# A two-layer diffusion block: the token stages put in source order, with the scan rewritten as a pipeline

## The chip, the cores and the metric

The kernel runs on one core of a Trainium2 chip. A core has a matrix engine (PE, whose weight loads are listed as PEld), a vector engine (DVE), a scalar engine (ACT), a general engine (POOL) and an engine that here only issues transfers (SP); each runs its own list of instructions from the first to the last, and they meet through semaphores. SBUF is the core's working memory, PSUM holds the matrix engine's sums. The metric is device microseconds of one execution.

## The reference, cut to what matters

Two layers are computed over 1024 latent and 256 context tokens of width 1024. Per layer:

```python
u = rmsnorm(h, g_pre) * (1 + sc) + sh                 # modulated, latent and context
p = split_proj(u @ w_in)                              # xbc, z, dt | gq gk gv gg | dq dk dv dg
y_s = ssd(p)       # xs,B,C = silu(dwconv(xbc)); scan in both directions, chunks of 128:
                   #   y_diag = (C B^T . exp(segsum(dt a))) (x dt)     inside a chunk
                   #   S_next = S * exp(sum dt a) + B (decay x dt)     state between chunks
                   #   y_off  = C S exp(cumsum dt a)                   state into the chunk
                   # y = yf + flip(yb) + x * d_skip; rmsnorm(y * silu(z)) * norm_g
y_g = attention(rope(norm(gq)), rope(norm(gk)), gv) * silu(gg)
y_d = norm(att(q1, k1, v) - lam * att(q2, k2, v)) * silu(dg)
h = h + gate * rmsnorm(concat(y_s, y_g, y_d) @ w_out, g_post)
```

The second layer needs no context output. All is float32 in and out; products are made of a high and a low part of each factor, so that one product is three matmuls.

## The kernel before, in words

The 1280 tokens are ten tiles of 128 (0 and 1 are context). Each layer goes through a stage with features on partitions (the convolution's channels), a **token stage**, the attention and the output projection. This text is about the token stage: 206 to 603 us in the first layer, 1273 to 1614 us in the second.

In it the rest of `w_in` is multiplied tile by tile, in five column blocks that the code calls chunks, in the order 0 (z), 1 (q and k of the differential attention), 3 (its v, 256 wide), 2 (q, k, v of the grouped attention), 4 (the gates); the others are 512 wide. A tile's product is eight k-steps of three matmuls into a PSUM tile `prj` (L958 to L960); `tok_chunk` first loads a chunk's weights and splits them (`wh`, `wl`), and then takes each tile from `prj` to `raw` (L977) and on: rotary (L879 to L888), in chunk 2 also a norm (squares L895, sums L897, an inverse root on POOL L117, the multiplication L899), the split in two parts `st` (L830 to L834), transposes `qps` (L841) and the store. In chunks 0 and 4 a tanh gate `th` (L963, L964) is stored through a ring of two buffers (`gt` or `z`, L965).

Beside chunks 0, 1 and 3 runs `scan()`, whose `yield`s are taken 1.3 times per 512-wide product. Per scan chunk it loads `xbf`, `ab` and `bct`; makes `gp` (L767) and from it `gf`; two DVE operations per head make the decay D (L773, L774), ACT its exponential (L776); eight copies on ACT (L779) and eight DVE operations (L780) make W, POOL multiplies W by D (L782), and PE multiplies by x (`pd`, L790). The state of either direction is decayed in place on POOL (L718), increased by `stp` (L714, L720) and read by `po` (L726, scaled L728). Outputs of the two directions are added when the second one comes to a tile, through partial sums in DRAM (`d_yp`, then `d_ys`). `finish()` (L731) reads that sum and z, and does gate, norm, transposes and the store; it is called on every second tile of chunks 2 and 4.

What stands in the program in this way is only a set of priorities: the whole kernel is put in order by a list scheduler, which simulates the engines and takes at each point the ready instruction with the best priority. On every engine the order is then fixed.

Of the kernel before, what the change touches and what calls it, by code (L numbers as in the profile page):

```python
# [48 lines left out]
SCR = 1.3  # L49
# [18 lines left out]
def block_kernel(ctx: ExitStack, tc: tile.TileContext, tok, cvec, wmod, pack,  # L68
# [61 lines left out]
    def cs(c):  # L130
        return slice(c * P, (c + 1) * P)
# [297 lines left out]
    for l in range(DEPTH):  # L429
# [15 lines left out]
        d_yp = dp.tile([NT, P, 512], F32, name=f"yp{l}")  # L445
        d_ys = dp.tile([NT, P, 512], F32, name=f"ys{l}")
# [8 lines left out]
        pk = lt_([P, NPK - NPM], "pk")  # L455
# [249 lines left out]
        def state_step(c, dr, xb, S, first):  # L705

            xs = sp.tile([P, 2, 256], F32, name="xs", tag="xs")
            G.tensor_tensor(xs.rearrange("p g (h d) -> p g h d", h=4),
                            xb[:, :, 0:256].rearrange("p g (h d) -> p g h d", h=4),
                            coef[:, dr, c, :].rearrange("p (g h) -> p g h", g=2).unsqueeze(3)  # L710
                            .to_broadcast([P, 2, 4, 64]), op=ALU.mult)
            ps = xpp.tile([P, 2, 256], F32, name="stp", tag="st")
            for g in range(2):
                TE.matmul(ps[:, g], xb[:, g, 256:384], xs[:, g], start=True, stop=True)  # L714
            if first:
                V.tensor_copy(S, ps)
            else:
                G.tensor_tensor(heads(S.rearrange("p g x -> p (g x)")), heads(S.rearrange("p g x -> p (g x)")),  # L718
                                per_head(etot, dr, c), op=ALU.mult)
                V.tensor_add(S, ps, S)  # L720

        def y_off(c, dr, bc, S):
# [4 lines left out]
            yt = sp.tile([P, 512], F32, name="yt", tag="yt")  # L727
# [3 lines left out]
        def finish(c, fp, nb=2):  # L731

            y = fp.tile([P, 512], F32, name="yf", tag="yf", bufs=nb)
            SY.dma_start(y, d_ys[c])
            zt = fp.tile([P, 512], F32, name="zt", tag="zt", bufs=nb)
            SY.dma_start(zt, d_z[c])
            V.tensor_tensor(y, y, zt, op=ALU.mult)
            sa = small.tile([P, 1], F32, name="sa")
            S_.activation(zt, y, AF.Square, accum_out=sa)
            rr = inv_root(sa, [P, 1], 1.0 / 512, 4 * EPS, "s")  # L740
            V.tensor_scalar(y, y, rr, None, op0=ALU.mult)
            pt = trp.tile([P, 4, P], F32, name="ytp", tag="tr")
            for i in range(4):
                TE.transpose(pt[:, i], y[:, cs(i)], ident)
            z3 = zt.rearrange("p (k t) -> p k t", k=4)
            V.tensor_tensor(z3, pt, pc("ssdg").unsqueeze(2).to_broadcast([P, 4, P]), op=ALU.mult)
            yp = fp.tile([P, 4, 2, P], F32R, name="yp2", tag="yp2", bufs=1)
# [4 lines left out]

        def scan():
            half = set()
            Sf = sp.tile([P, 2, 256], F32, name="Sf")
            Sb = sp.tile([P, 2, 256], F32, name="Sb")
            for c, cb in enumerate((1, 0, 9, 8, 7, 6, 5, 4, 3, 2)):
                xb = sp.tile([P, 2, 384], F32, name="xbf", tag="xb", bufs=2)
                SY.dma_start(xb, d_xb[c])
                if c >= t0:  # L760
                    ab = sp.tile([P, 2, 8, P], F32, name="ab", tag="ab")
                    SY.dma_start(ab, d_acs[:, c].unsqueeze(0).to_broadcast([P, 2, 8, P]))
                    bc = sp.tile([P, 4, P], F32, name="bct", tag="bct", bufs=2)
                    SY.dma_start(bc, d_bc[:, :, cs(c)].rearrange("i p t -> p i t"))
                    pg = xpp.tile([P, 2, P], F32, name="gp", tag="gp")
                    for g in range(2):
                        TE.matmul(pg[:, g], bc[:, 2 * g], bc[:, 2 * g + 1], start=True, stop=True)  # L767
                    gf = sp.tile([P, 2, 2, P], F32, name="gf", tag="gf")
                    V.tensor_tensor(gf[:, 0], pg, mge.unsqueeze(1).to_broadcast([P, 2, P]), op=ALU.mult)
                    V.tensor_tensor(gf[:, 1], pg, mle.unsqueeze(1).to_broadcast([P, 2, P]), op=ALU.mult)  # L770
                    D, W = ab[:, 0], ab[:, 1]
# [5 lines left out]
                    yield  # L777
                    for h in range(8):
                        S_.activation(W[:, h], gf[:, 0, h // 4], AF.Copy, scale=dts[:, 0, c, h:h + 1])  # L779
                        V.scalar_tensor_tensor(W[:, h], gf[:, 1, h // 4], dts[:, 1, c, h:h + 1], W[:, h],  # L780
                                               op0=ALU.mult, op1=ALU.add)
                    G.tensor_tensor(W, W, D, op=ALU.mult)  # L782
                    y = sp.tile([P, 512], F32, name="y", tag="y", bufs=2)
                    G.tensor_tensor(y.rearrange("p (g h d) -> p g h d", g=2, h=4),
                                    xb[:, :, 0:256].rearrange("p g (h d) -> p g h d", h=4),
                                    pc("dskip").rearrange("p (g h) -> p g h", g=2).unsqueeze(3)
                                    .to_broadcast([P, 2, 4, 64]), op=ALU.mult)
                    pd = xpp.tile([P, 8, 64], F32, name="pd", tag="pd")
                    for h in range(8):
                        TE.matmul(pd[:, h], W[:, h], xb[:, h // 4, h % 4 * 64:h % 4 * 64 + 64],  # L790
                                  start=True, stop=True)
                    V.tensor_tensor(y, pd.rearrange("p h d -> p (h d)"), y, op=ALU.add)
                    if c:
                        yt = y_off(c, 0, (bc[:, 1], bc[:, 3]), Sf)
                        G.tensor_tensor(y, yt, y, op=ALU.add)
                    if c in half:
                        yt = sp.tile([P, 512], F32, name="yp", tag="yp")
                        SY.dma_start(yt, d_yp[c])
                        G.tensor_tensor(y, yt, y, op=ALU.add)
                    whole = c in half or c == 1  # L800
                    half.add(c)
                    SY.dma_start((d_ys if whole else d_yp)[c], y)
                    yield
                if c != NT - 1:
                    state_step(c, 0, xb, Sf, c == 0)
                xb = sp.tile([P, 2, 384], F32, name="xbb", tag="xb", bufs=2)
                SY.dma_start(xb, d_xb[cb])
                if c and cb >= t0:
                    ct = sp.tile([P, 2, P], F32, name="ct", tag="ct")
                    SY.dma_start(ct, d_bc.rearrange("(g b) p t -> b p g t", b=2)[1][:, :, cs(cb)])  # L810
                    yt = y_off(cb, 1, (ct[:, 0], ct[:, 1]), Sb)
                    if cb in half:
                        y = sp.tile([P, 512], F32, name="y", tag="y", bufs=2)
                        SY.dma_start(y, d_yp[cb])
                        G.tensor_tensor(y, yt, y, op=ALU.add)
                        SY.dma_start(d_ys[cb], y)
                    else:
                        half.add(cb)
                        SY.dma_start(d_yp[cb], yt)
                if cb != 2:  # L820
                    state_step(cb, 1, xb, Sb, c == 0)
# [68 lines left out]
        def gqa_norm(ck, raw, parts, t):  # L890
# [3 lines left out]
            sq = ck.tile([P, nh, 64], F32, name="gsq", tag="t2", bufs=T2B)  # L894
            S_.activation(sq, raw3, AF.Square)  # L895
# [13 lines left out]
        with pool("rot") as rp, pool("tokc", 2) as ck:  # L909
# [29 lines left out]
            def tok_chunk(ck, ch, first):  # L939
# [11 lines left out]
                for t in range(first, NT):  # L951
# [26 lines left out]
                    if ch == 1:  # L978
                        if t >= 2:
                            rope(ck, raw, 16, 16, cosd[:, t - 2], nsind[:, t - 2], sind[:, t - 2], False)  # L980
# [641 lines left out]
```

## Time and profile before

| | |
|---|---|
| median of 3 runs | 2064.58 us (2062.05 to 2068.44) |
| profiled execution, its own time | 2063.46 us |
| its span in the trace | 2061.6 us |
| mean granted clock of PE | 0.937 |
| busy in the span | PE 88%, PEld 71%, DVE 69%, POOL 59%, ACT 51% |
| token stages | 397.1 us in layer 0, 341.6 us in layer 1 |

The stages are cut at these times: chunks 0, 1 and 3 with the scan, then chunk 2, then chunk 4. In the stage view a line gives the stretch, its length, the busy time of PE, PEld, DVE, ACT and POOL with the number of instructions, then the granted clock of PE (1.00 is its upper level), the busy share of the transfer engines and GB/s. In a list of waits a line says which instruction stood and for which, the total, the number of times and the longest one. A name such as `ab` is a tile of the program.

### The profile page before, as it was taken

To read this page: it belongs to the slowest core of one execution; us is meant where nothing else is said; L and a number is where in the kernel's file an instruction comes from. 1 tells how busy PE (TensorE), PEld (TensorE's weight loads), DVE (VectorE), ACT (ScalarE), POOL (GpSimd) and SP (SyncE) were. 2 spreads that over 40 slices of the span, in tenths; PEclk is the share of its full clock that TensorE was granted. 3 is DMA by queue.
4 is the path that set the end of the run, shared out by engine and by line. 5 is a ranking of instruction groups with operands and counts; after the bars stand their busy time and mean duration, and the time that the engine had idled before them with its cause. 6 is when DMAs were issued, how large, how long until landed. Compare 5 with 4: busy or idle time off the path is not lost. (4 is left out here: it accounts for less than half of the span.)

```text
span 2061.6 us, 30333 instructions
## 1 busy us (share of the span) xinstructions
PE 1806.6 (88%) x9936; PEld 1471.4 (71%) x9936; DVE 1428.5 (69%) x3286; ACT 1041.5 (51%) x1955; POOL 1211.7 (59%) x1135
## 2 busy tenths in 40 slices
PE   4899989899879999988988799888899899989895
PEld 3677777787668667876775487777777777878783
DVE  4777566766538776698866578468656588788954
ACT  3445233334437775766654345234244477777661
POOL 3626245747616676777755326466567378787761
PEclk9899999899999999998989899999999999999897
DMA  9157546776786788786656138667766866557545
GB/s 290 47 170 271 152 165 191 236 235 176 222 259 198 245 263 257 234 256 202 211 191 214 63 102 280 226 183 231 244 202 204 260 185 192 157 155 237 161 152 205
DMA packets 359998, 418.57 MB, mean 203 GB/s; under 512 B 38753, under 2 KB 252833, under 8 KB 359841
## 3 DMA queue, kind: packets, MB, share of 16 engines
q1 hardware_dynamic: 359840, 416.64, 65.1%
q8 instruction: 78, 1.28, 0.3%
q14 instruction: 80, 0.65, 0.1%
HBM read 282.18 MB, written 134.38 MB: 202 GB/s over the span
## 5 line engine op out<-in xcount | busy, mean ns | idle before, releaser
L128 POOL TENSOR_TENSOR pl<-pf,ph 128x512 fp32r<-128x512 f32 x283 | 373.6, 1325 | 189.0 <-DVE ph L1391 69.7
L1241 DVE TENSOR_SCALAR_CACHE_REDUCE pt<-sc 128x512 f32<-128x512 f32 (+1 forms) x600 | 334.2, 587 | 78.5 <-PE sc L1239 63.4
L958 PE MATMUL prj<-wh,u 128*128 128x512 f32 (+1 forms) x768 | 296.6, 389 | 33.0 <-DVE th L964 18.1
L1254 ACT ACTIVATE pt<-pt,nm 128x1280 f32<-128x1280 f32 x192 | 262.3, 1366 | 92.1 <-DVE nm L1252 91.0
L959 PE MATMUL prj<-wl,u 128*128 128x512 f32 (+1 forms) x768 | 294.8, 384 | 10.3 <-POOL wl L128 7.8
L960 PE MATMUL prj<-wh,u 128*128 128x512 f32 (+1 forms) x768 | 291.7, 380 | 0.0
L1369 PE MATMUL tp<-ident,pt 128*128 128x128 f32 x1312 | 209.3, 285 | 14.0 <-ACT pt L1254 5.6
L1379 ACT COPY pf<-tp 128x512 f32<-128x512 f32 x289 | 166.8, 581 | 74.9 <-PE tp L1369 49.3
L1412 PE MATMUL po<-pl,vt 128*128 128x256 f32 x644 | 183.1, 307 | 15.6 <-POOL pl L128 14.7
L958 PEld LDWEIGHTS prj<-wh,u 128*128 128x128 f32 x768 | 151.8, 199 | 62.5 <-DVE th L964 19.9
L1411 PE MATMUL po<-ph,vt 128*128 128x256 f32 x644 | 186.0, 303 | 5.2 <-DVE ph L1391 2.9
L1369 PEld LDWEIGHTS tp<-ident,pt 128*128 128x128 f32 x1312 | 162.1, 147 | 37.9 <-ACT pf L1379 10.7
L959 PEld LDWEIGHTS prj<-wl,u 128*128 128x128 f32 x768 | 152.0, 198 | 38.0 <-POOL wl L128 11.2
L960 PEld LDWEIGHTS prj<-wh,u 128*128 128x128 f32 x768 | 151.7, 198 | 23.5
L1239 PE MATMUL sc<-dk,q 128*128 128x512 f32 (+1 forms) x400 | 146.1, 408 | 15.2 <-DVE pt L1241 12.0
L1412 PEld LDWEIGHTS po<-pl,vt 128*128 128x128 f32 x644 | 126.3, 196 | 33.0 <-POOL pl L128 25.3
L1411 PEld LDWEIGHTS po<-ph,vt 128*128 128x128 f32 x644 | 127.2, 197 | 19.4 <-DVE ph L1391 5.6
L606 DVE SCALAR_TENSOR_TENSOR cacc<-craw,hw,cacc 128x1284 f32<-128x1284 f32 (+1 forms) x64 | 120.0, 1877 | 28.0 <-ACT cacc L603 12.0
L581 PE MATMUL prj<-u,wTh 128*128 128x512 f32 x256 | 109.8, 429 | 22.2 <-DVE u L209 14.2
L1239 PE MATMUL sc<-gk,q 128*128 128x256 f32 (+1 forms) x400 | 110.0, 385 | 19.9 <-DVE pt L1241 16.7
L342 PE MATMUL ops<-y,wo 128*128 128x512 f32 (+1 forms) x304 | 117.7, 387 | 10.5 <-DMA y<-y 6.3
L582 PE MATMUL prj<-u,wTh 128*128 128x512 f32 x256 | 109.3, 427 | 7.4 <-DVE u L128 6.8
(277 smaller groups left out, 4310.7 us busy)
## 6 DMA issues: line engine op xcount, KB each, us to landing
wo<-wo SPq DMA_DIRECT2D x80, 512.0 KB, 4.9
wm<-in_wmod_dram SPq DMA_DIRECT2D x48, 512.0 KB, 6.2
dk<-dk SPq DMA_DIRECT2D x16, 1280.0 KB, 7.9
ab<-acs SPq DMA_DIRECT2D x18, 1024.0 KB, 7.5
wo<-wos SPq DMA_DIRECT2D x32, 512.0 KB, 3.7
wf<-in_wtok_dram SPq DMA_DIRECT2D x64, 256.0 KB, 4.4
y<-y SPq DMA_DIRECT2D x30, 512.0 KB, 5.7
op<-o SPq DMA_DIRECT2D x48, 256.0 KB, 4.4
```

Of the source, the lines that this page charges most:

```text
L128: eng.tensor_tensor(out_, full, hi.bitcast(F32), op=ALU.subtract)
L606: V.scalar_tensor_tensor(acc[:, a0:1284], raw[:, a0 + j:1284 + j], hw[:, i * 5 + j:i * 5 + j + 1], acc[:, a0:1284], op0=ALU.mult, op1=ALU.add)
L958: TE.matmul(ps[:, c0:], uh, wh[k][:, c0:], start=k == 0, stop=False)
L959: TE.matmul(ps[:, c0:], uh, wl[k][:, c0:], start=False, stop=False)
L960: TE.matmul(ps[:, c0:], ul, wh[k][:, c0:], start=False, stop=k == KT - 1)
L1239: TE.matmul(ps[:, 0:b - a].rearrange("p (t c) -> p t c", c=P), q[:, jb.q0 + j], kt[:, a // P:b // P], start=x == 0, stop=x == len(qq) - 1)
L1241: V.tensor_scalar(ts[r][:, a:b], ps[:, 0:b - a], -1.0, None, op0=ALU.mult, op1=ALU.min, accum_out=mts[r][:, i:i + 1])
L1254: S_.activation(e, e, AF.Exp, bias=nm, scale=-1.0, accum_out=jb.s2[:, j, mp_:mp_ + 1])
L1369: TE.transpose(tp[:, j * P:(j + 1) * P], jb.pt[2 * hf + j % 2][:, cs(2 * s + j // 2)], ident)
L1379: S_.copy(pf[:, :w_], tp[:, :w_])
L1411: TE.matmul(o, vv, a[:, c], start=k == 0, stop=False)
L1412: TE.matmul(o, vv, b[:, c], start=False, stop=k == jb.nk - 1)
```

## The change

From the first weights of the token stage to its last product PE, DVE, ACT and POOL keep the order in which the source names their instructions; SP's transfers are still placed by the scheduler, as is the rest of the kernel. The source itself is laid out anew:

- `scan()` has three steps per scan chunk. Step A: `gp` and the forward `po` of this chunk and `pd` of the chunk before, `gf`, `yt`, the sum of `pd`, then D, its exponential, x times d_skip, the decayed forward state. Step B: `stp` forward, the sum into the state, W, the decayed backward state, W times D. Step C: `po` and `stp` backward. Transfers are asked for a step or more ahead, `ab` has two buffers instead of one, `bct` one instead of two, and `xbf` and `xbb` have tags of their own.
- The decayed state is a tile of its own, `sd`, rather than the state itself. Forward and backward outputs go to `d_yf` and `d_yb`, and `finish` adds them.
- A tile's work after its product (`tok_rows`) is a generator, each piece of which is taken one product later than the one before, by `rest`. The first two tiles of a chunk are multiplied together, k-step by k-step. The weights of the next chunk are loaded and split while the last product of the current one runs.
- `finish` is a generator of eight pieces; up to two run at once in chunk 2, three in chunk 4. The first two tiles of the gates are multiplied before chunk 2's last pieces.
- The rotary tables of the grouped attention are made at the start of chunk 2, no longer ahead of chunk 0.

The same number of instructions stands on each engine in both kernels. The core of the diff:

```diff
-        def state_step(c, dr, xb, S, first):
+        def state_decay(c, dr, S):
+            Sd = sp.tile([P, 2, 256], F32, name="sd", tag="xs", bufs=2)
+            G.tensor_tensor(heads(Sd.rearrange("p g x -> p (g x)")), heads(S.rearrange("p g x -> p (g x)")),
+                            per_head(etot, dr, c), op=ALU.mult)
+            return Sd
...
+            for c, cb in enumerate(CB + (None,)):
...
+                if left:
+                    xl, wl_, yl, cl = left
+                    pd = xpp.tile([P, 8, 64], F32, name="pd", tag="pd")
+                    for h in range(8):
+                        TE.matmul(pd[:, h], wl_[:, h], xl[:, h // 4, h % 4 * 64:h % 4 * 64 + 64],
+                                  start=True, stop=True)
...
+                if mid:
+                    G.tensor_tensor(W, W, D, op=ALU.mult)
+                if c < NT - 1:
+                    ahead = load(c + 1)
+                yield
...
+            def product(ch, group, beside):
...
+                pss = [prj.tile([P, 512], F32, name="prj", tag="prj")[:, 0:w_] for _ in group]
+                pss_of[ch, group] = pss, c0
+                ks = [(i, k - i) for k in range(KT + 1) for i in range(len(group)) if 0 <= k - i < KT]
+                at = [len(ks) * n // len(beside) for n in range(len(beside))]
+                for n, (i, k) in enumerate(ks):
+                    while at and at[0] == n:
+                        at.pop(0)
+                        beside.pop(0)()
...
+            def rest(ck, ch, group, more=None):
+                on(pipe[0])
+                if more:
+                    next(more)
+                on(pipe[1])
+                finish_on()
+                if more:
+                    next(more, None)
+                on(pipe[1])
+                finish_on()
+                done = pipe.pop(0)
+                new = []
+                if group:
+                    pss, c0 = pss_of.pop((ch, group))
+                    new = [tok_rows(ck, ch, ps, t, c0) for ps, t in zip(pss, group)]
+                    on(new)
+                pipe.append(new)
+                on(done)
...
+            tok_order.enter_context(tc.manual_schedule(engines={E_.PE, E_.DVE, E_.Activation, E_.Pool}))
+            for _ in tok_weights(0):
+                pass
             with pool(f"ssd{l}") as sp:
                 sc = scan()
-                credit = 0.0
-                for ch in (0, 1, 3):
-                    for _ in tok_chunk(ck, ch, t0 if ch == 0 else 0):
-                        credit += SCR * CW[ch] / 512
...
+                rate, credit = 32 / (units - SCD - 1.0), 0.0
...
+                product(4, groups(4)[0], [])
+                while running or pipe[0] or pipe[1]:
+                    rest(ck, 2, None)
```

PE in the middle of a product of chunk 1, first layer, before; `u_101` and so on are the eight k-steps of the input:

```order
L960 MATMUL prj<-wh,u_101 128x512
L958 MATMUL prj<-wh,u_102 128x512
L959 MATMUL prj<-wl,u_102 128x512
L726 MATMUL po<-Sb,ct 128x256 x2
L714 MATMUL stp<-xs,xbb 128x256 x2
L841 MATMUL qps<-identr,st 128x128 x8
L790 MATMUL pd<-xbf,ab 128x64 x8
L960 MATMUL prj<-wh,u_102 128x512
```

The scheduler put the backward step, the transposes and a scan chunk's `pd` in one place, with `pd` of the scan chunk whose W was just made. The same engine and chunk after the change:

```order
L1110 MATMUL prj<-wh,u_101 128x512
L831 MATMUL gp<-bct 128x128 x2
L735 MATMUL po<-Sf,bct 128x256 x2
L838 MATMUL pd<-xbf,ab 128x64 x8
L1108 MATMUL prj<-wh,u_102 128x512
L1109 MATMUL prj<-wl,u_102 128x512
L1110 MATMUL prj<-wh,u_102 128x512
```

`gp` and `po` of a new scan chunk and `pd` of the one before now stand together in the middle of a product; the `stp`s stand at other steps.

ACT in chunk 2 of the first layer before, where `gsq` is a tile's squares, `st` the high part after its rotary, `raw` the copy out of PSUM and `tt` the copy of its transposes:

```order
L977 COPY raw<-prj 128x512
L990 CAST vs<-raw 128x2x64
L895 ACTIVATE gsq<-raw 128x384
L843 COPY tt<-qps 128x512
L843 COPY tt<-qps 128x256
L834 CAST st<-raw 128x6x64
L977 COPY raw<-prj 128x512
```

A tile's squares come at a point that varies from tile to tile. After the change:

```order
L1054 COPY raw<-prj 128x512
L918 COPY tt<-qps 128x512
L918 COPY tt<-qps 128x256
L909 CAST st<-raw 128x6x64
L1072 CAST vs<-raw 128x2x64
L969 ACTIVATE gsq<-raw 128x384
L1054 COPY raw<-prj 128x512
```

One period per tile now repeats: the `st` of a tile stands directly ahead of the `vs` and `gsq` of the tile after it, and then comes the copy of the tile after that.

## Rows read from the trace of the kernel before

**Rows 1.** Token stages: us, busy (count) PE PEld DVE ACT POOL; clock, DMA.
```profile
206.00:452.80 246.80, 219.83 (x1142) 186.96 (x1141) 156.31 (x349) 79.73 (x178) 122.08 (x96) 0.92 0.62 190
452.80:522.80 70.00, 65.22 (x319) 52.21 (x319) 43.48 (x94) 28.99 (x70) 50.54 (x59) 1.00 0.66 198
522.80:603.10 80.30, 66.56 (x290) 52.35 (x288) 31.45 (x55) 23.22 (x52) 32.97 (x41) 0.91 0.80 241
1272.90:1490.10 217.20, 187.13 (x1037) 160.28 (x1036) 141.79 (x293) 73.08 (x162) 124.11 (x98) 0.94 0.72 221
1490.10:1556.90 66.80, 61.16 (x311) 50.61 (x309) 38.43 (x87) 27.60 (x68) 47.60 (x59) 0.95 0.68 205
1556.90:1614.50 57.60, 53.48 (x235) 42.23 (x234) 29.11 (x50) 20.01 (x44) 30.18 (x37) 0.91 0.74 218
```

**Rows 2.** Two stretches around a wait for POOL, columns as in rows 1.
```profile
363.20:370.00 6.80, 5.14 (x29) 4.14 (x27) 5.17 (x15) 2.36 (x6) 5.64 (x3) 1.00 0.75 204
370.20:376.90 6.70, 6.27 (x26) 5.73 (x27) 2.09 (x3) 1.68 (x4) 6.70 (x7) 0.50 0.45 107
```

**Rows 3.** Waits of PE, 206 to 452.8 us: total, times, longest.
```profile
PE po L726 <- DVE yt L728: 5.2, 2, 4.3
...
PE gp L767 <- DMA bct<-bc: 2.8, 1, 2.8
```

**Rows 4.** Waits of PE, 452.8 to 603.1 us.
```profile
PE prj L958 <- DVE th L964: 8.6, 2, 7.0
PE prj L959 <- POOL wl L128: 4.7, 4, 2.2
PE prj L958 <- ACT wh L947: 1.5, 1, 1.5
```

**Rows 5.** Waits of PE, 1490.1 to 1614.5 us.
```profile
PE prj L958 <- ACT wh L947: 4.3, 3, 3.5
PE prj L959 <- DVE wl L128: 2.3, 3, 1.1
```

**Rows 6.** The diagonal products by line, 240 to 480 us: ns min/median/max.
```profile
L790 PE MATMUL pd<-xbf,ab x160: 217/275/473, 248.3 to 475.9; 128*128 128x64 f32 x160
```

**Rows 7.** Timeline of PE, one token tile's product: start, duration.
```profile
1514.20 0.39 PE L958 MATMUL prj<-wh,u 128*128 128x512 f32 x1
...
1519.64 0.39 PE L958 MATMUL prj<-wh,u 128*128 128x512 f32 x1
```

**Rows 8.** Chunk 1 of layer 0, columns as in rows 1.
```profile
290.80:394.60 103.80, 90.62 (x431) 74.52 (x431) 66.63 (x158) 38.08 (x88) 57.22 (x47) 0.92 0.68 200
```

**Rows 9.** Groups of instructions on POOL, 206 to 452.8 us: busy, mean ns.
```profile
L782 POOL TENSOR_TENSOR ab<-ab 128x1024 f32<-128x1024 f32 x9 | 23.4, 2595 | 23.3 <-DVE ab L780 23.3
```

**Rows 10.** Timeline of one tile's norm and rotary in chunk 2.
```profile
487.55 0.53 ACT L895 ACTIVATE gsq<-raw 128x384 f32<-128x384 f32 x1 [5.46 <-POOL raw L888]
...
489.04 1.33 POOL L117 TENSOR_TENSOR nrr<-irm,mhalf 128x6 f32<-128x6 f32 x1
...
490.34 1.01 POOL L128 TENSOR_TENSOR st<-raw,st 128x384 fp32r<-128x384 f32 x1
...
490.41 1.36 DVE L899 TENSOR_TENSOR raw<-raw,nrr 128x384 f32<-128x384 f32 x1 [1.74 <-POOL nrr L117]
...
491.31 0.78 POOL L128 TENSOR_TENSOR vs<-raw,vs 128x128 fp32r<-128x128 f32 x1
...
494.35 0.51 ACT L834 CAST st<-raw 128x384 fp32r<-128x384 f32 x1
```

**Rows 11.** The norm's multiplication by line: ns min/median/max.
```profile
L899 DVE TENSOR_TENSOR raw<-raw,nrr x20: 293/688/1652, 474.4 to 1588.7; 128x384 f32<-128x384 f32 x18, 128x128 f32<-128x128 f32 x2
```

**Rows 12.** Waits of ACT, 522.8 to 603.1 us.
```profile
ACT th L963 <- DMA gt<-th: 17.0, 2, 16.3
```

**Rows 13.** Timeline of SP's queue in the gates' stage.
```profile
568.05 0.43 SPq L1042 DMA_DIRECT2D gk<-gk  x1
...
587.51 0.38 SPq L965 DMA_DIRECT2D gt<-th  x1
```

More of the change, by code (lines that the diff above doesn't have):

```diff
@@ L764, in scan, with load_back @@
[L764 to L767, printed above, removed]
+                return xf, ab, bc
+            def load_back(c):
+                xb = sp.tile([P, 2, 384], F32, name="xbb", tag="xbb")
+                SY.dma_start(xb, d_xb[CB[c]])
+                ct = None
+                if c and CB[c] >= t0:
+                    ct = sp.tile([P, 2, P], F32, name="ct", tag="ct")
+                    SY.dma_start(ct, d_bc.rearrange("(g b) p t -> b p g t", b=2)[1][:, :, cs(CB[c])])
+                return xb, ct
@@ new lines, in scan @@
+            ahead = load(0)
+            back = load_back(0)
+            yield
+            xs = state_in(0, 0, ahead[0])
+            left = None
+            for c, cb in enumerate(CB + (None,)):
+                if c < NT:
+                    xf, ab, bc = ahead
+                    mid = c >= t0
+                    if mid:
+                        pg = xpp.tile([P, 2, P], F32, name="gp", tag="gp")
+                        for g in range(2):
+                            TE.matmul(pg[:, g], bc[:, 2 * g], bc[:, 2 * g + 1], start=True, stop=True)
+                        if c:
+                            po = y_off((bc[:, 1], bc[:, 3]), Sf)
+                if left:
[4 more added lines that the diff above has]
+                                  start=True, stop=True)
+                if c < NT and mid:
@@ L781, in scan @@
                                                op0=ALU.mult, op1=ALU.add)
+                    if c:
+                        G.tensor_tensor(y, yt, y, op=ALU.add)
+                Sd = state_decay(cb, 1, Sb) if c and cb != 2 else None
+                if mid:
                     G.tensor_tensor(W, W, D, op=ALU.mult)
[L783 to L819, printed above, removed]
@@ new lines, in on @@
+            def on(gens):
+                for g in gens:
+                    next(g, None)
+            def rest(ck, ch, group, more=None):
[16 more added lines that the diff above has]
+                on(done)
@@ L1108, in block_kernel @@
             vt[(0, 0)] = load_v(d_dv, 0, "dv", 2)
-            for t, _ in enumerate(tok_chunk(ck, 4, t0)):
-                if t % 2 and todo:
-                    finish(todo.pop(0), ck, GNB)
-            while todo:
-                finish(todo.pop(0), ck, GNB)
+            for n, group in enumerate(groups(4)):
+                if n:
+                    product(4, group, [])
+                finish_new(ck, 3)
+                rest(ck, 4, group)
+            while running or todo:
+                finish_new(ck, 3)
+                finish_on()
+        tok_order.close()
         tks.close()
```

298 lines of the change are left out of this document (190 added, 108 removed).

## The prediction

> **What bounds the kernel now.** I read the stage view first, because the share of the whole span mixes stages. In the six token stages PE is the busiest engine in every line, and none of the others comes near it [rows 1]: in the first stage PE is busy 219.8 of 246.8 us, DVE 156.3, POOL 122.1, ACT 79.7. So time can be won in two places only: where PE stands idle, and where its granted clock is below 1.00. Stage by stage, length less PE's busy time gives the idle time, and one less the granted clock, times the length, gives what the clock cost. In the order of the rows the idle times are 27.0, 4.8, 13.7, 30.1, 5.6 and 4.1 us (together 85.3), the clock's losses 19.7, 0, 7.2, 13.0, 3.3 and 5.2 us (48.4). The ceiling of this change is thus about 134 us of the token stages' 738.7, if the same work were done without a gap at full clock.
>
> The two losses hang together. In a stretch in which PE was idle 1.7 of 6.8 us the clock was at its upper level (1.00, 2.4 GHz); in the 6.7 us after it it stood at 0.50 (1.2 GHz), although PE was busy 6.3 us of them [rows 2]. So a microsecond of idle time costs more than itself: 19.7/27.0, or 0.73 us on top in the first stage, 0.43 in the fourth, 0.53 in the third.
>
> Next the places of the waits. With the scan, PE waits in `po` for `yt` (5.2 us in two waits) and at the start for `bct` (2.8 us) [rows 3]; the rest is spread over many small ones. In the last two stages of layer 0 it waits for the gates' buffers (8.6 us) and for the weights' split (4.7 and 1.5 us) [rows 4], in those of layer 1 for the weights alone (4.3 and 2.3 us are the two largest) [rows 5].
>
> **The scan's stage.** Engine work is equal in both kernels, so nothing is removed but waits. The ten sets of `pd` start between 248.3 and 475.9 us [rows 6], one scan chunk each 25 us. What must PE do in it? The first stage at full clock without gaps is 246.8 - 27.0 - 19.7 = 200.1 us. It holds 25 products of 512 columns (ten, ten, and ten of half width), at 5.44 us each, which is the distance from one product's first matmul to the next one's [rows 7]: 136 us. The other 64 us are the scan and the transposes, 6.4 us for each of ten scan chunks. The new loop takes 32 steps over 22 products, 1.45 steps per product where it was 1.3, so a scan chunk lies beside 2.06 products: 2.06 x 5.44 + 6.4 = 17.6 us of PE. DVE has 66.6 us in chunk 1 [rows 8], 6.7 per product; 2.06 of them are 13.7, and with the scan 1.12 times as dense at most 15.4 us. PE stays the longest, by 2 us. The chain through the other engines fits too: POOL's multiplication of W by D, 2.6 us [rows 9], now stands at the end of step B, and `pd` reads it in step A of the next scan chunk, with step C, a third of a period or 5.9 us, between. In the old order `pd` came soon after its W.
>
> What idle time is left I add up from waits that the new order doesn't take away: the start, where `gp` now stands in PE's list ahead of the products and needs `bct` (2.8 us, as before); one meeting of PE and DVE such as that at `po` (5.2 us, as before); two changes of chunk, half of the 6.2 us that weights cost elsewhere [rows 4], since they now load beside the last product (3 us); and the scan's last steps with no product beside them, one step (5.9 us). Together 17 us instead of 27.0 and 30.1. Bounds: 0 and the old values, or above them (rival two). With each stage's own loss of clock per idle time, layer 0 has 10.0 + 7.3 = 17.3 us less, and layer 1 13.1 + 5.7 = 18.8. Sum: -36 us. Two `ab` buffers, the `sd` tile and the separate outputs cost nothing here beyond this: they are the same instructions, and the loads' cover is the step that they are ahead. If that cover goes, it is the 2.8 us of `bct` again, per scan chunk.
>
> **Chunk 2.** Here the fixed order makes a loop. ACT does `st` of a tile, then `vs` and `gsq` of the next one; and that tile's `st` needs its `gsq`, the sums, the root on POOL, the multiplication, the rotary and POOL's addition. In the trace the way from `gsq` (487.55) to `st` (494.35) is 6.8 us [rows 10]. With `st` itself (0.51) and some 0.3 us for `vs` the loop is 7.6 us per tile. POOL's way is no longer: from `st` on, its two low parts (1.01 and 0.78 us) end about when the sums are there. PE needs 65.2/10 = 6.5 us per tile [rows 1], the old order took 7.0 in layer 0 and 6.7 in layer 1. Eight single tiles in the loop are 61 us, the first pair 10.9: 72 us against 70.0. In layer 1 the first pair is keys only, about half: 66.5 against 66.8. The last tiles' way out lies beside the gates' first pair, 10.9 us of PE, as it did in the scheduler's order. Bounds: PE alone sets the pace, which takes off the idle time and clock loss of these stages (4.8 and 8.9 us); or the loop grows by a second root of POOL, that of `finish`, 1.33 us, and by the slowest multiplication (1.65 instead of 1.36 us [rows 11]), to 9.2 us, 8 x 2.2 = 18 us more per layer. I take 0, which is where the timeline of one tile puts it.
>
> The multiplication by the root took 1.36 us from 490.41 on, while POOL worked on `st`'s low part from 490.34 to 491.35; the median of this line is 0.69 us [rows 10, 11]. The Trainium skill, page "SBUF — State Buffer", section "Who interferes with whom" and the part on the two sides ahead of it, says that a DVE operation with two SBUF inputs and a GpSimd operation that reads SBUF hold a shared port pair in turn, and that the later one stands until the other is done. The trace agrees. In the new order that low part is ahead of the root and can't meet the multiplication; by the rule alone the loop would be 6.9 us, and the forecast 11 us lower. The pieces of `finish` can meet it instead, so I leave the row's value.
>
> **The gates.** In layer 0 the weights' 4.7 and 1.5 us [rows 4] go, since they load beside chunk 2's last product and the first pair is multiplied ahead: 6.2 x 1.53 = 9.5 us. The 8.6 us for `th` stay: ACT stands 17.0 us for the store of a gate [rows 12], because SP issues the attention's loads ahead of that store (from 568.05 to 587.51 us [rows 13]), and neither SP's placing nor the ring of two is changed. In layer 1 the weights' 6.6 us [rows 5] go too, 12.4 us with the clock's part (8.5 us for 9.7 idle in these two stages); but the pair that is now multiplied early fills the ring, and the loads can stand ahead of its stores as in layer 0, which costs 7.0 us with its clock, up to 13. I take 0, between -12 and +13.
>
> **Sum.** -36 + 0 - 9.5 + 0 = -45.5 us, against the profiled execution's own 2063.5 us: 2018. The median of the runs is 1.1 us above that execution, so I forecast 2019 us.
>
> **Rivals.** *One: the stalls go nearly all.* The pipeline is laid so that every operand is ready a step early; then two thirds of the 134 us go, 89 us, and the time is 1976 us. For it speaks that PE has 2 us more per period than DVE; against it that starts, chunk changes and the gates' stores have no cover, and that a short wait also lowers the clock.
>
> *Two, on the other side: the fixed lists close loops through POOL and ACT.* The list scheduler placed each instruction when it was ready in its simulation; now an instruction that waits holds all that stands behind it on its engine. In the scan's stage POOL has five multiplications per scan chunk and each tile's addition and low part behind one another, and ACT holds PE's next PSUM buffer behind eight copies and an exponential. If this way round stays at the old 25 us, the 36 us are not won; and the loop of chunk 2 at 9.2 us adds 2 x 18. With the gates at -5 that is 2064.6 + 36 - 5 = 2096 us. It decides from a scan period of 23 us and a tile period of 8 on. For it: ACT does stand 17.0 us in one place, with products behind it [rows 12]; against it: the periods worked out above are 17.6 and 7.6 us. The Trainium skill, "PSUM — Partial Sum Buffer", section "Engine vs sequencer instructions", states that these engines' queues are strictly in order; how much stands behind such a wait in the new order, no row here shows.
>
> *Three: what the scan wins, chunk 2 gives back.* Scan -36, chunk 2 +36, gates -5: 2060 us, no change. The same comes out where the simulated order was already as good as the written one, for which speaks that the old waits are many and small.
>
> **How the numbers follow.** The forecast has 0.58, rival one 0.14, rival two 0.15, rival three 0.13. A measurement of this kernel can tell about 0.3%, 6 us. Faster holds the forecast and rival one, 0.72; same is rival three, 0.13; slower is rival two, 0.15. The likeliest case's own range, from its bounds in the scan's idle time (some 14 us either way) and in chunk 2 and the gates (13 and 13 us), is 1995 to 2045 us. To hold 8 in 10 the range takes in rival three and half of rival one: 1980 to 2072 us.
>
> **What would show it.** Right: a first stage near 230 us and a fourth near 198, sets of `pd` 18 to 20 us apart, PE's idle time there near 17 us, and a granted clock of 0.94 to 0.97; chunk 2 as long as before, with ACT's `gsq` standing for POOL's addition by way of `st`; weights' waits gone in the gates, `th`'s wait left. Wrong: `pd` sets 25 us apart; DVE busier than PE in chunk 1's periods; a tile of chunk 2 over 8 us; or a change outside the token stages, of which the sum has none.

## The result, and the profile after

The changed kernel takes 2189.22 us (median of 4 runs, 2185.99 to 2191.51) against 2066.51 us before (4 runs): 1.0593 times as long, 95% interval 1.0565 to 1.0621. The span grew from 2061.6 to 2186.1 us, and the granted clock fell from 0.937 to 0.917. The forecast was 2019 us.

The stage view of the changed kernel, columns as in [rows 1]: the six stages of [rows 1], then chunk 1 of layer 0, as in [rows 8].

```profile
201.40:482.30 280.90, 227.66 (x1165) 192.76 (x1165) 167.86 (x375) 81.14 (x188) 111.09 (x90) 0.90 0.57 174
482.30:568.10 85.80, 65.79 (x306) 52.74 (x305) 42.68 (x79) 28.32 (x67) 52.13 (x67) 0.92 0.53 157
568.10:657.80 89.70, 66.53 (x275) 53.39 (x274) 32.43 (x46) 20.90 (x45) 33.52 (x40) 0.83 0.71 206
1336.30:1595.40 259.10, 203.55 (x1061) 173.40 (x1060) 156.45 (x315) 74.65 (x171) 114.55 (x93) 0.88 0.61 193
1595.40:1670.60 75.20, 59.54 (x299) 49.57 (x298) 41.60 (x77) 26.03 (x65) 50.40 (x68) 0.91 0.55 169
1670.60:1745.60 75.00, 54.42 (x218) 43.43 (x218) 24.87 (x38) 17.14 (x37) 26.58 (x32) 0.82 0.70 198
287.90:431.60 143.70, 106.44 (x485) 86.80 (x485) 86.87 (x191) 39.90 (x95) 66.29 (x54) 0.86 0.54 163
```

Every one of the six stages is longer, 865.7 us together where they were 738.7: 127 us, the whole loss. The two stages with the scan are 76 us longer (34.1 and 41.9), chunk 2 is 24 us longer in the two layers, the gates 27 us. In chunk 1 of layer 0 no engine is busy more than 74% of 143.7 us; DVE and POOL have 60% and 46%. So nothing is full: PE waits more, and its clock is lower. (The 103.8 us that chunk 1 took before are no measure for it: the new source puts more of the scan there, 80 multiplications `pd` where there were 50. The first experiment below has the same work in the scheduler's order.)

PE's waits in the scan's stage of layer 0, after (total, times, longest; to compare with [rows 3]):

```profile
PE qps L916 <- DVE st L906: 15.5, 4, 4.5
PE qps L916 <- POOL st L128: 12.5, 6, 3.4
PE prj L1108 <- DVE th L1042: 8.9, 1, 8.9
PE prj L1108 <- ACT raw L1054: 6.3, 2, 4.3
PE gp L831 <- DMA bct<-bc: 3.0, 1, 3.0
```

The first two were small in the kernel before, whose two rows are these:

```profile
PE qps L841 <- DVE st L831: 4.0, 3, 1.6
PE qps L841 <- POOL st L128: 0.2, 1, 0.2
```

Now a tile's transposes `qps` stand in PE's list in front of the next product, and their `st` is late. The wait for `bct` is the one of before.

**The first place: a ring in chunk 1.** One turn of it, from the timeline after (start, duration), left out are, among others, the products and thirteen of the sixteen operations of the decay:

```profile
359.67 1.89 PE L838 MATMUL pd<-xbf,ab 128*128 128x64 f32 x16
...
361.60 0.69 DVE L847 TENSOR_TENSOR y<-pd,y 128x512 f32<-128x512 f32 x1 [1.04 <-PE pd L838]
...
362.21 0.28 DVE L854 TENSOR_SCALAR ab<-ab,acs 128x128 f32<-128x128 f32 x1
362.52 0.35 DVE L855 SCALAR_TENSOR_TENSOR ab<-ab,acs 128x128 f32<-128x128 f32 x1
...
366.61 0.35 DVE L855 SCALAR_TENSOR_TENSOR ab<-ab,acs 128x128 f32<-128x128 f32 x1
367.00 1.06 ACT L857 ACTIVATE ab<-ab 128x1024 f32<-128x1024 f32 x1 [13.68 <-DVE ab L855]
367.96 0.40 ACT L905 ACTIVATE st<-raw 128x256 fp32r<-128x256 f32 x1
...
368.39 0.43 DVE L906 SCALAR_TENSOR_TENSOR st<-raw,st 128x256 fp32r<-128x256 f32 x1 [1.43 <-ACT st L905]
...
368.87 0.62 PE L916 MATMUL qps<-identr,st 128*128 128x128 f32 x3 [4.53 <-DVE st L906]
```

PE does `pd` in the middle of a product. Only then can DVE add it (361.60), and the whole decay stands behind that addition; ACT's exponential stands behind the decay, the tile's `st` on ACT behind the exponential, its low part on DVE behind that, and PE's transposes behind all of it. That is 9.2 us from `pd` to `qps`, while the rest of the product gives PE work for 2.8 us after `pd`: it stands 4.53 us. Of what follows the decay only the exponential needs it; the order of the lists alone ties a tile's split to it. The other half of the period has the same form over W, POOL's multiplication (2.4 to 3.1 us) and the low part behind it on POOL (waits of 2.5 to 3.4 us). One such place:

```profile
348.48 2.51 POOL L880 TENSOR_TENSOR ab<-ab 128x1024 f32<-128x1024 f32 x1 [2.92 <-DVE ab L874]
...
350.95 0.90 POOL L128 TENSOR_TENSOR st<-raw,st 128x256 fp32r<-128x256 f32 x1
...
351.91 0.62 PE L916 MATMUL qps<-identr,st 128*128 128x128 f32 x3 [2.48 <-POOL st L128]
```

**The second place: the change of chunk.** The stage of chunk 2 in layer 0, ACT after:

```profile
486.81 0.62 ACT L1031 CAST wh<-wf 128x512 fp32r<-128x512 f32 x1 [5.23 <-DMA wf<-in_wtok_dram]
488.14 1.30 ACT L1031 CAST wh<-wf 128x512 fp32r<-128x512 f32 x2 [0.71 <-DMA wf<-in_wtok_dram]
492.85 1.27 ACT L1031 CAST wh<-wf 128x512 fp32r<-128x512 f32 x2 [3.41 <-DMA wf<-in_wtok_dram]
494.03 0.36 ACT L1048 CAST vs<-prj 128x256 fp32r<-128x256 f32 x1
```

And PE there, released by DVE's low part, which follows the copy:

```profile
494.91 0.80 PE L1108 MATMUL prj<-wh,u 128*128 128x512 f32 x1 [11.02 <-DVE vs L128]
```

The last product of chunk 3 is copied out of PSUM (`vs<-prj`) only after the eight casts of the next weights (the last five are in these rows), since `rest` names the weights first; the casts wait for their loads; and the pair that opens the chunk needs both PSUM buffers. PE stands 11.0 us here, 8.9 us at the start of chunk 1, 4.3 us at that of chunk 3 and 8.7 us at that of the gates; in layer 1 11.0 and 8.8 us are the longest two. In the kernel before, the scheduler had put this copy between the casts, four ahead of it and four behind:

```profile
453.88 0.62 ACT L947 CAST wh<-wf 128x512 fp32r<-128x512 f32 x1 [3.57 <-DMA wf<-in_wtok_dram]
454.41 0.37 ACT L971 CAST vs<-prj 128x256 fp32r<-128x256 f32 x1
454.68 0.62 ACT L947 CAST wh<-wf 128x512 fp32r<-128x512 f32 x1
```

### The profile page after: what moved, and what is told of

The parts are those of the page before. It is cut to its first block, busy times and chain, and to the rows that moved or that the text cites. A ratio compares the mean times of both kernels' runs of the same rounds, so it can differ in the third digit from the quotient of the medians.

```text
span 2186.1 us, 30317 instructions
## 1 busy us (share of the span) xinstructions
PE 1830.2 (84%) x9936; PEld 1491.7 (68%) x9936; DVE 1445.2 (66%) x3286; ACT 1035.7 (47%) x1955; POOL 1194.0 (55%) x1135
## 5 line engine op out<-in xcount | busy, mean ns | idle before, releaser
L1108 PE MATMUL prj<-wh,u 128*128 128x512 f32 (+1 forms) x768 | 310.3, 404 | 88.1 <-DVE th L1042 37.0
L1110 PE MATMUL prj<-wh,u 128*128 128x512 f32 (+1 forms) x768 | 292.5, 381 | 0.0
L1108 PEld LDWEIGHTS prj<-wh,u 128*128 128x128 f32 x768 | 156.5, 204 | 118.7 <-DVE th L1042 38.6
L1110 PEld LDWEIGHTS prj<-wh,u 128*128 128x128 f32 x768 | 155.3, 202 | 26.5
L1393 PE MATMUL sc<-dk,q 128*128 128x512 f32 (+1 forms) x400 | 141.4, 403 | 14.0 <-DVE pt L1395 11.2
L581 PE MATMUL prj<-u,wTh 128*128 128x512 f32 x256 | 108.9, 425 | 20.9 <-DVE u L209 13.8
```

Of the source, the lines that this page charges most:

```text
L1108: TE.matmul(ps[:, c0:], uh, wh[k][:, c0:], start=k == 0, stop=False)
L1110: TE.matmul(ps[:, c0:], ul, wh[k][:, c0:], start=False, stop=k == KT - 1)
L1393: TE.matmul(ps[:, 0:b - a].rearrange("p (t c) -> p t c", c=P), q[:, jb.q0 + j], kt[:, a // P:b // P], start=x == 0, stop=x == len(qq) - 1)
```

## The experiments

In the table a chunk's length runs from its first product's first matmul to that of the next chunk (of the gates, to the last matmul), from the profiled execution of each kernel; `none` has the new source with no list fixed. Ratio is to the kernel before as it was measured beside each, with its interval; rows compare best by it.

| lists fixed | median us | ratio | chunks 0, 1, 3, 2, 4 of layer 0 | of layer 1 |
|---|---|---|---|---|
| (kernel before) | 2066.5 | | 85 104 58 70 79 | 65 96 56 67 57 |
| none | 2060.6 | 0.9975 (0.9946 to 1.0004) | 85 107 53 70 72 | 58 121 43 70 56 |
| PE | 2115.3 | 1.0234 (1.0215 to 1.0253) | 98 111 49 84 76 | 69 110 51 82 57 |
| DVE | 2127.9 | 1.0299 (1.0281 to 1.0318) | 82 105 68 71 92 | 62 98 77 67 80 |
| ACT | 2110.2 | 1.0194 (1.0153 to 1.0235) | 83 110 49 84 83 | 56 113 56 80 69 |
| PE, DVE | 2130.6 | 1.0299 (1.0261 to 1.0338) | 87 120 46 87 79 | 68 120 51 79 67 |
| PE, ACT, POOL | 2158.2 | 1.0445 (1.0425 to 1.0466) | 94 130 47 88 86 | 66 132 51 76 74 |
| DVE, ACT, POOL | 2189.5 | 1.0592 (1.0567 to 1.0618) | 98 139 53 83 86 | 64 132 65 73 71 |
| all four | 2189.2 | 1.0593 (1.0565 to 1.0621) | 87 144 51 86 90 | 68 138 53 75 75 |

The scheduler can also move work from one chunk to another, so a single chunk's length is a fair measure only where the order on all engines is fixed, or where the work in it is known to be the same.

**Order or rewrite?** (`none`, the scheduler for all engines)

```diff
-            tok_order.enter_context(tc.manual_schedule(engines={E_.PE, E_.DVE, E_.Activation, E_.Pool}))
```

> The new source with the scheduler ordering all engines again (the fixed order alone taken out). Theory A (the fixed lists close loops through ACT and DVE, the rewritten scan and the prefetched weights cost nothing): near the kernel before, 2030 to 2080 us, with PE's waits at the transposes under 10 us in each layer instead of 39 and 35. Theory B (the rewrite itself costs, by separate outputs, more traffic and the decayed state in its own tile): most of the loss stays, 2140 us or more.

Measured: 2060.57 us. Theory B falls: the separate outputs, `sd`, the prefetched weights and the new pipeline cost nothing, and win nothing that can be told. The whole loss is the fixed order. Chunk 1 of layer 0, with the same 80 multiplications `pd`, takes 107.2 us in this kernel, and DVE is busy 85% of them:

```profile
286.60:393.80 107.20, 96.59 (x486) 81.24 (x485) 91.34 (x183) 38.57 (x94) 66.17 (x54) 0.94 0.63 191
```

The same work in the fixed order takes 143.7 us.

**The copy ahead of the weights.** In `rest`:

```diff
                 if more:
+                    evac()
                     next(more)
...
-                if group:
+                if group and not more:
+                    evac()
```

> One thing moved: at a chunk's end the copy of the last product out of PSUM stands on ACT ahead of the eight casts of the next chunk's weights, not behind them. Theory A: PE's long waits at each chunk's second tile (8.9, 11.0 and 8.7 us in layer 0, about 26 us in layer 1) go, with their share of the clock 60 to 80 us: 2110 to 2130 us. Theory C (PE is late everywhere because DVE and POOL are full, and waits in the next place instead): under 25 us won, 2165 us or more.

`evac()` is what stood further down in `rest`: it takes the product's tiles to `tok_rows` and starts their work with the copy. Measured: 2182.50 us, ratio 1.0576 (1.0536 to 1.0617). Theory A's price fails. The wait of 11.0 us at the start of chunk 2 is 1.5 us, and those of 8.9 and 8.7 us are gone, but PE waits elsewhere, and the whole can't be told from the changed kernel's 1.0593. The same span of the program as above, layer 0, in this kernel:

```profile
PE qps L916 <- DVE st L906: 20.9, 6, 4.5
PE qps L916 <- POOL st L128: 12.7, 6, 3.4
PE stp L725 <- POOL xs L708: 7.3, 1, 7.3
```

Waits for DVE's `st` grew from 15.5 to 20.9 us, `stp` stands 7.3 us for POOL's `xs`, and chunk 3 of layer 1 is 64.5 instead of 53.4 us.

**The transposes a product later**, alone and with the former move:

```diff
+                on(late)
                 on(pipe[0])
...
-                on(done)
+                late[:] = done
```

> One thing moved: a tile's transposes and their copies stand one product later, on PE and on ACT. Theory A: PE's waits for st (39 us in layer 0, 35 us in layer 1) fall under 10 us, chunk 1 falls from 144 and 138 us to about 110, the whole to 2090 to 2120 us. Theory C: DVE's list sets chunk 1's period of 28 us for two products, PE waits in a product's start instead, and the time stays over 2160 us.

> Both moves together. Theory A: the two add up, 2030 to 2060 us, and what is left over the kernel before stands in the gates and in chunk 2. Theory C: 2130 us or more.

Measured: 2223.07 us, ratio 1.076 (1.072 to 1.080), and 2189.34 us, 1.0602 (1.0559 to 1.0645). Both against theory A: chunk 1 of layer 0 falls, but only to 132 us, and there PE stands in another place. PE's largest wait in chunk 1 with the transposes late:

```profile
PE po L735 <- DVE yt L740: 12.8, 3, 4.7
```

`po` has one PSUM buffer, emptied by `yt`, which stands on DVE behind the low part of `st`, which waits for ACT. The next link of the same lists took the place of the broken one. With the transposes alone moved, chunks 3, 2 and 4 of layer 0 got 8.5, 5.4 and 7 us longer; with both moves what chunk 1 won was lost mainly in chunk 3 (57 and 74 us where it was 51 and 53).

**Which lists?** The set in one line, here for PE alone; the table has the results.

```diff
-            tok_order.enter_context(tc.manual_schedule(engines={E_.PE, E_.DVE, E_.Activation, E_.Pool}))
+            tok_order.enter_context(tc.manual_schedule(engines={E_.PE}))
```

> Only PE keeps the source order, the scheduler orders DVE, ACT and POOL. Theory D (PE and DVE, each in a fixed list, wait for each other by turns; with one of the two free the turn is broken): 2060 to 2090 us, waits of PE at the transposes under 15 us in layer 0. Theory E (it is PE's list alone, with transposes and scan steps at fixed places of a product, that stands): most of the loss stays, 2140 us or more.

> DVE, ACT and POOL keep the source order, the scheduler orders PE. Theory D: 2060 to 2100 us, since PE can go on with the next product while st is late. Theory E: about 2060 us as well. Theory F (the lists of the side engines are late by themselves, whatever PE does): 2140 us or more.

> PE, ACT and POOL keep the source order, the scheduler orders DVE. Theory D: 2060 to 2100 us. Theory E: 2140 us or more. Theory G (the turn is closed by ACT, where st stands behind the exponential and the copies out of PSUM behind st): 2140 us or more too, with ACT's waits as long as with all four fixed.

> Only DVE keeps the source order. Theory D: 2060 to 2090 us. Theory F: a large part of the loss, 2110 us or more, because the decay of a scan chunk (3.75 us of DVE) then stands ahead of a tile's rotary and split.

> Only ACT keeps the source order. Theory G (ACT's list is what closes the turns: st behind the exponential that waits for DVE, and the copies out of PSUM behind st): a large part of the loss alone, 2120 us or more, with chunk 1 of layer 0 at 125 us or more. Theory H (no list does it alone, the loss needs PE or DVE fixed beside it): under 2100 us, chunk 1 under 112 us.

> PE and DVE keep the source order, the scheduler orders ACT and POOL. PE alone cost 55 us over no fixed list, DVE alone 67. Theory D (PE and DVE wait for each other by turns): more than the sum of the two, near all four, 2170 us or more, chunk 1 near 140 us. Theory G: chunk 1 under 115 us, the whole near the larger of the two or their sum, 2130 to 2170 us.

Against `none` each of the three lists costs some 45 to 67 us alone by the ratios, each elsewhere: PE in chunks 0 and 2 (98 and 84 us instead of 85 and 70), ACT in chunk 2 and the gates (84 and 83 instead of 70 and 72), DVE in chunk 3 and the gates. In chunk 1 of layer 0 no list alone does much (105 to 111 us). PE and DVE together make 120 us there, three lists with ACT and POOL among them 130 and 139, all four 144. So theory D is too narrow: PE and DVE together give 2131 us, not 2170, and with DVE free it is still 2158. Theory E falls, since freeing PE alone wins nothing (2189.5 us), and that run is what theory F said of the side engines. Theory G falls for ACT alone (110 us in chunk 1, 2110 in all, a little over theory H's 2100), but not for ACT and POOL beside PE. So no one list is needed for the loss: it comes with PE, ACT and POOL in source order without DVE, and with DVE, ACT and POOL without PE. That each of these sets closes a ring of its own is the likely reading, and not shown; and POOL's list was never fixed alone.

**The split a product earlier**, chunk 1:

```diff
                         rope(ck, raw, 16, 16, cosd[:, t - 2], nsind[:, t - 2], sind[:, t - 2], False)
                     yield
-                    yield
                     if konly:
```

> All four fixed; in chunk 1 a tile's split into st stands one product earlier, so that it no longer stands behind the next scan step's decay and exponential, and its transposes are where they were. Theory A (the turn PE, DVE, ACT, DVE, PE by way of st): the 4.5 us waits at the transposes go, chunk 1 falls from 144 to about 115 us, the whole to 2130 us. Theory G (another turn takes its place, as with the transposes moved): chunk 1 stays over 130 us and PE waits at po or at a product's start instead.

Measured: 2194.70 us, ratio 1.0603 (1.0563 to 1.0643); chunk 1 is 136.5 us. The long waits at the transposes went as theory A said, but chunk 1 won only 7 us, and theory G's sentence came true: PE's largest wait in that chunk is

```profile
PE po L735 <- DVE yt L740: 15.6, 3, 6.3
```

**A third buffer for the transposes' copies**, on top of the two moves (`tag="tt", bufs=3`):

> The two moves of before (copy out of PSUM ahead of the weights, transposes one product later) and a ring of three instead of two buffers for the transposes' copies. In the run with the two moves ACT stood 3.2 and 2.0 us for those buffers' stores, DVE behind it for st, PE behind DVE at po. Theory I (the stores close that turn): chunk 1 falls from 132 us to about 115, the whole by 20 us or more to under 2170 us. Theory C: no change, 2180 us or more.

Measured: 2181.83 us, ratio 1.0542 (1.0495 to 1.0589) beside 1.0602 without it; chunk 1 130.5 instead of 131.7 us. Theory I falls: the stores were not what closed that turn.

**A ring, or work?** One link of the ring made shorter; that is, half of the decay's operations on DVE are left out:

```diff
                     for h in range(8):
-                        V.tensor_scalar(D[:, h], D[:, h], acs[:, 0, c, h:h + 1], None, op0=ALU.subtract)
```

> All four lists fixed; of a scan chunk's decay on DVE the first eight of sixteen operations (the subtraction) are left out, some 2.5 us per scan chunk, in both layers. Theory A (a ring of waits through the four lists sets chunk 1's pace, 30.0 us per scan chunk, with DVE busy 60% of it): the period falls by the whole 2.5 us, PE's waits for st behind the decay from 4.5 to 2.0 us, chunk 1 from 144 to about 131 us, the whole by 20 to 35 us. Theory C (PE is held by work that fills it, or by transfers): under 8 us in the whole, PE not being busy with this.

Measured: 2152.30 us, ratio 1.0412 (1.0380 to 1.0443), 37 us less than with all four fixed and a little more than the 20 to 35 that were expected. Chunk 1 falls from 143.7 to 130.3 and from 138.0 to 119.0 us. PE's waits in chunk 1 of layer 0, of this kernel (lines are one lower):

```profile
PE qps L915 <- POOL st L128: 9.9, 5, 3.4
PE prj L1107 <- DVE th L1041: 9.1, 1, 9.1
PE qps L915 <- DVE st L905: 8.8, 5, 2.5
```

The waits of 4.53 us behind the decay are 1.90 to 1.96 us (the sum counts one of 2.5), 2.6 us shorter, the 2.5 us that eight operations take; the waits for POOL, on the ring's other half, stay at 3.4. Two scan chunks that were 30.0 us apart are 26.8 and 27.4 us apart. DVE was idle 40% of that chunk, so a lighter load on DVE is no explanation: the way from `pd` over the decay to `qps` sets the period, link by link. This is shown for that half. The half over POOL is read from the timeline; no run shortened it.

**Can the freed source gain?**

```diff
-                rate, credit = 32 / (units - SCD - 1.0), 0.0
+                rate, credit = 1.3, 0.0
...
-                    if n >= SCD - 1:
+                    if True:
...
+                    if ch == 3:
+                        tok_order.close()
```

The old rate (the first two pieces) is in the first and the third of these kernels; DVE's list alone, given back to the scheduler before chunk 3 (the last piece), in the second and the third.

> No fixed list, and the scan's steps taken 1.3 times per product from the first product on, as before, where the new source takes 1.45 after a delay. The new rate packs the scan denser into chunk 1 (107 and 121 us with no fixed list against 104 and 96 before). Theory J (that density is what keeps the freed kernel from gaining): chunk 1 of layer 1 under 105 us, the whole 2035 to 2050 us. Otherwise no change, 2055 to 2065 us.

> Only DVE fixed, and only through chunks 0 and 1, where that alone took 105 and 99 us in chunk 1; from chunk 3 on the scheduler orders all. If stages add up: chunks 0 and 1 187 and 160 us, chunk 3 near 53 and 45, the rest as with no fixed list: 2035 to 2050 us. If DVE's fixed order only pushes scan work into chunk 3 (it took 68 and 77 us there): 2065 us or more.

> The same with the old rate of 1.3 steps per product from the first product on. If both gains are there and add: 2030 to 2045 us. If the fixed DVE list makes the rate indifferent: as the run with DVE fixed through two chunks, within 6 us.

Measured: 2069.15 us with no list fixed and the old rate, ratio 1.0001 (0.9981 to 1.0021); 2101.84 us, 1.0169 (1.0138 to 1.0200), with DVE fixed through chunks 0 and 1; 2105.59 us, 1.0184 (1.0155 to 1.0213), with both. Theory J falls, and so does adding up stages: with DVE fixed in two chunks, chunk 1 is 107 and 102 us, but chunk 3 after it is 69 and 78 us where it was 53 and 43, although the scheduler orders it. None of these beats the kernel before clearly; the nearest is `none`.

## Why the prediction was wrong, point by point

- **The bounding engine and the ceiling** were read rightly for the kernel before: PE, and only its waits and its clock. What failed is that the new order was taken only to remove waits: the term "together 17 us" for PE's idle time in either scan stage came out at 53 and 56 us, and its idle time in the six stages went from 85 to 188 us (lengths less busy time). The sum had -36 us for the scan stages, 0 for chunk 2 and -9.5 for the gates; they came out at +76, +24 and +27.
- **The step that failed** is "PE stays the longest, by 2 us". The period of a scan chunk was taken as the largest of the engines' sums of work, 17.6 us. Without a tile's rotary and split beside it that is near: in chunk 0 the sets of `pd` are 16.7 us apart. In chunk 1, once rotary and split run beside the scan, they are 30.0 to 31.8 us apart. A settled period, from one set of `pd` to the next:

```profile
359.67:389.67 30.00, 21.90 (x102) 17.84 (x100) 18.73 (x40) 7.92 (x19) 14.14 (x11) 0.89 0.54 157
```

  Of this PE stands 4.53 and 3.40 us, and its clock is halved for 6.8 us, which costs about 3.4: the remaining 18.7 us are its work, near the forecast sum. DVE was to have at most 15.4 us and has 18.7, so it is level with PE; but either sum is far below 30.0. The sums were not the bound. In a fixed order the bound here is a closed way through the lists, and "the chain through the other engines fits too" followed only the data, W to `pd`, not the neighbours in the lists: a tile's `st` behind the exponential, and that behind the whole decay.
- **Changes of chunk** were put at 3 us of idle time for the two beside the scan, and at nothing for the other two. The prediction saw that weights now load beside the last product, but not that eight casts stand in ACT's list ahead of the copy that frees PSUM: 8.9 and 4.3 us beside the scan, 11.0 and 8.7 us after it, in layer 0. Moving that copy won nothing that can be told, so they are not worth their sum: other waits took their place.
- **A row of the kernel before was left out.** The prediction names 5.2 us for `yt` and 2.8 us for `bct` and calls the rest many small waits. The largest wait of that stage was another one, at 311.08 us in chunk 1, for a copy out of PSUM on ACT:

```profile
PE prj L958 <- ACT raw L977: 5.4, 1, 5.4
```

  That copy (310.47 us) stood on ACT behind a cast that had waited 7.45 us for its load, behind copies of W and behind the exponential. It is the same kind of wait that the new order made many of.
- **Chunk 2** was followed as a ring, and there the period came out nearly: 7.96 to 8.15 us per tile from 526 to 558 us, forecast 7.6, and at the 8 us from which rival two was to decide. One turn is from `gsq` at 534.38 us to `gsq` at 542.34. On POOL an addition of `finish` follows the root:

```profile
534.38 0.52 ACT L969 ACTIVATE gsq<-raw 128x384 f32<-128x384 f32 x1
...
536.13 1.33 POOL L117 TENSOR_TENSOR nrr<-irm,mhalf 128x6 f32<-128x6 f32 x1
537.44 1.29 POOL L756 TENSOR_TENSOR yf<-yf,yb 128x512 f32<-128x512 f32 x1
537.50 1.64 DVE L978 TENSOR_TENSOR raw<-raw,nrr 128x384 f32<-128x384 f32 x1 [2.02 <-POOL nrr L117]
...
542.34 0.52 ACT L969 ACTIVATE gsq<-raw 128x384 f32<-128x384 f32 x1
```

  The multiplication takes 1.64 us, beside POOL's addition in place of the low part. The Trainium skill, "SBUF — State Buffer", section "Who interferes with whom", says that a DVE instruction with two SBUF inputs contends with a GpSimd instruction that reads SBUF. The trace agrees: at 577.13 us, where POOL was idle, the same multiplication took 0.55 us. The shorter loop that the low part's move could have given did not come, as the prediction allowed for. Chunk 2 is 15.8 us longer in layer 0 and 8.4 in layer 1; 11.0 us of idle time stand at the change of chunk in either.
- **The gates** were to win 9.5 us in layer 0. The weights' waits did go (none is left among PE's long ones), those for `th` stayed in layer 0 (12.2 us in two waits, 8.6 before) and came up in layer 1 (9.5 us), which the prediction had named as a risk and taken as 0. With the change of chunk (8.7 and 8.8 us) and the lower clock (0.83 and 0.82) the stage is 9 and 17 us longer.
- **Rival two** had the mechanism, lists that close loops, with a chance of 0.15 and 2096 us. Its price was too low because it let the scan keep the old period of 25 us and knew nothing of the changes of chunk: it had 0 for the scan's stages, 36 for chunk 2 and -5 for the gates, where +76, +24 and +27 us came out.

What stays open: whether the half of the ring over POOL sets the period as the other half does; why moving one link (the transposes, the split, the copy) costs as much in other stages, chunk 3 above all, as it wins in chunk 1; and why DVE's list alone lengthens chunk 3 and the gates. How much of the loss lies in SP's order of the transfers, which was still the scheduler's and made for other times, was not tried by itself.

## What to carry to other kernels

Engine sums give the floor of a pipeline in fixed lists, not its period: write down each list for one period, and follow every wait to the neighbour ahead in the list, round until it comes back. Here such a round took 1.6 times the fullest engine's work (30.0 us against 18.7). Look above all at an operation that frees a PSUM buffer behind one that may wait for a load, and at one tile's output behind another task's long block. But moving one of them may only move the wait to the next: here no such move won anything that could be told, and one lost. So try the new source with the order left to the scheduler first (here 2061 us against 2189), and look for the round's second longest way before counting on a sum.

## What the runs showed of the hardware

In this kernel a short wait cost PE its clock soon after. The stage view around the 4.53 us wait, after: up to the wait's end, behind it, and further on.

```profile
360.00:368.80 8.80, 4.34 (x26) 3.52 (x25) 6.05 (x20) 1.80 (x4) 0.01 (x1) 1.00 0.68 224
368.90:372.20 3.30, 3.13 (x13) 2.58 (x14) 1.81 (x3) 2.40 (x7) 2.10 (x2) 0.50 0.30 68
372.40:381.70 9.30, 5.96 (x28) 4.57 (x27) 8.60 (x13) 2.83 (x8) 7.65 (x6) 1.00 0.51 133
```

While PE stood, the granted clock was at its upper level, 2.4 GHz; in the 3.3 us in which it worked again it was at 1.2 GHz, and then back. In chunk 1 of layer 0 a stretch at 1.2 GHz went with each of PE's seven longest waits (2.5 to 8.9 us); with two of them it began while PE still stood. So two waits of 8 us together in a period cost about 11.

DVE also takes longer beside POOL in the ring itself. The eight operations for W took 0.35 us each from 346.00 us on, while POOL was idle. From 373.09 us on the first three took 0.61, 1.38 and 1.13 us beside operations on POOL, and the other five 0.34. The product for the rotary at 378.41 us took 2.71 us beside POOL's multiplication, where it took 0.69 at 370.05. No run tried what this costs the period.
